# Third modulation round taken from the gated products into three heads, with its weights packed in order of use

## The chip, the core and the metric

The kernel runs on one core of one Trainium2 chip. The metric is the device time of one execution in microseconds; the median of several runs is given. Engines are named as in the profile: PE (TensorE matmul), PEld (TensorE weight load), DVE (VectorE), ACT (ScalarE), POOL (GpSimd), SP (SyncE, which issues most loads).

## What is computed

Two blocks of a network on 512 positions of width 1024. The change lies in the first one. All of it that matters here:

```python
cond = jax.nn.silu(c)
mod = cond @ ada_w[l] + ada_b[l]                       # (1, 6 * 1024)
sh1, sc1, g1, sh2, sc2, g2 = jnp.split(mod[:, None, :], N_MOD, axis=-1)
u = rms_norm(x, mix_pre_g[l]) * (1.0 + sc1) + sh1
proj = u @ w_in[l]                                     # heads (q, k, v, o), gates, glu
...                                                    # 4 heads of a chunkwise mLSTM
a, gt = jnp.split(glu, 2, axis=-1)
y = causal_dwconv(a * jax.nn.sigmoid(gt), cv_dw_w[l], cv_dw_b[l])   # 31 taps
y = jax.nn.silu(layer_norm(y, cv_ln_g[l], cv_ln_b[l]))
mix = jnp.concatenate([h, y], axis=-1) @ w_out[l]
x = x + g1 * rms_norm(mix, mix_post_g[l])
u = rms_norm(x, ffn_pre_g[l]) * (1.0 + sc2) + sh2
...                                                    # feed-forward part, uses g2 at its end
```

The second block (attention, memory cross-attention, mixture of experts) follows on the same core.

## The kernel before

**Order of the stages.** Memory keys and values (`memory`, to about 77 us), norm of x into u, the eight gated products (phase `glu`, c = 0 to 7), the gates, four heads (phases `qk`, `vo`, `mlstm`; h = 0 to 3), output product of the mixer (`wout`), feed-forward part, and then the second block. The program is straight-line. The order on each engine is set when it is built, by a scheduler that mostly follows the order of the code but takes an instruction earlier where its data should be ready.

**Modulation rounds.** `mod` has 6144 columns, in three rounds of 2048 (`ada_round`, r = 0, 1, 2). A round has eight steps, one for each 128 rows of `ada_w`. A step loads two tiles of 128 x 1024 floats (512 KB each, SP) and multiplies them with the condition in four matmuls (eight records in the profile, line L245), which lie in four column strips of PE and add up in one PSUM bank `pb` over all eight steps. At the end DVE adds the bias (L248) into `misc`. The tiles have four buffers, so two steps can be loaded ahead. Round 0 runs within the memory stage. Rounds 1 and 2 run within the gated products: there the tiles have the tag "qk" of the pool `pa`, and the biases lie in two tiles of that pool. The pool's space is that of the pool of the memory stage and is free once the last result of that stage is stored (`kvd`). c = 0, 1, 4, 5 take one step each, and c = 2, 3, 6, 7 take three.

**Weights of products.** `weight` loads 512 KB (tag "raw", three buffers, SP). In the stages around the change ACT writes the rounded high part (L133) and the negative raw value (L135) is made into the low part by an accumulating transfer that POOL issues (L136). The pairs have four buffers ("whl"). `fm_tile` makes one product of 128 x 512 outputs of them: 24 matmuls (L144, L145, L146). One c of the gated products is two such products, pg and pv, and DVE multiplies them to g (L647).

**Convolution.** The 31 taps over g are a generator: each step is one DVE instruction (L630) on an accumulator y. `pump(n)` issues n steps; `PUMP` says how many after each c (first eight numbers), each qk product (ninth) and each vo weight (tenth). What is left is issued at once by `drain` in head 3.

**Heads.** A head has four qk products, then four weights for v and the output gate (kk = 0 to 3, into four PSUM banks), the scores between them, and the matmuls with v (`mlstm_out`). The results of two heads lie in one half of hT.

**Large tiles.** xT (x transposed), u, hT and yT take two halves each of a tag "U" with four buffers (`U`, `Uh`), which rotate. `sh2` and `g2p`, columns of rounds 1 and 2, are taken in head 1.

Of the kernel before, what the change touches and what calls it, by code (L numbers as in the profile page):

```python
# [11 lines left out]
F32 = mybir.dt.float32  # L12
F32R = mybir.dt.float32r
# [3 lines left out]
ALU = mybir.AluOpType  # L17
PSUM = bass.MemoryType.PSUM

P = 128  # L20
# [26 lines left out]
class Kern:  # L47
    def __init__(self, ctx, tc, a, cidx):
        self.ctx, self.tc, self.nc, self.a, self.cidx = ctx, tc, tc.nc, a, cidx
        self.uid = 0  # L50
        self.phase = "a"
        self.bg = []

        self.lowdma = False
        self.turn = 0
# [36 lines left out]
    def Uh(self, dt):  # L92
        return self.p0.tile([P, 4, 2, 512], dt, tag="U", bufs=4, name=self.nm("U"))
# [135 lines left out]
    def ada_round(self, r, pool, tag, bias=None):  # L229

        nc = self.nc
        if bias is None:
            bias = self.tB()
        for j in range(4):
            o = r * 2048 + j * 512
            nc.sync.dma_start(bias[32 * j:32 * j + 32, :], self.a["ada_b"][0:1, o:o + 512].partition_broadcast(32))
        ps = self.psB()
        for k in range(8):
            w = []
            for j in range(2):  # L240
                t = pool.tile([P, 1024], F32, tag=tag, bufs=4, name=self.nm("aw"))
                nc.sync.dma_start(t, self.a["ada_w"][k * P:(k + 1) * P, r * 2048 + j * 1024:r * 2048 + (j + 1) * 1024])
                w += [t[:, :512], t[:, 512:]]
            for j in range(4):
                nc.tensor.matmul(ps[32 * j:32 * j + 32, :], self.crep[:, k, :], w[j], start=k == 0, stop=k == 7)  # L245
            yield
        self.mods[r] = self.misc[:, r % 2 * 512:r % 2 * 512 + 512]
        nc.vector.tensor_tensor(self.mods[r], ps, bias, op=ALU.add)  # L248
        yield
# [242 lines left out]
    def block1(self):  # L492
        nc, tc, a = self.nc, self.tc, self.a
        self.ada_setup()
        with tc.tile_pool(name="pz", bufs=1) as pz:
# [19 lines left out]
            ada = self.ada_round(0, pz, "aw")  # L515
# [13 lines left out]
            def weave(i):  # L529
                if i in (0, 2, 3, 5, 7, 9, 11, 13):  # L530
                    next(ada, None)
                if i == 13:
                    next(ada, None)
                if i in (3, 5, 7, 9):
                    x_load((3, 5, 7, 9).index(i))
                if i == 15:
                    norm1()
# [4 lines left out]
        with tc.tile_pool(name="pf", bufs=1) as pf:  # L542
# [4 lines left out]
            for tb in range(4):  # L547
                t = pf.tile([P, 1024], F32, tag="x4", bufs=6, name=self.nm("x"))
# [63 lines left out]
    def mixer(self, pa, u):  # L612
        nc, a = self.nc, self.a
# [20 lines left out]
        PUMP = (8, 9, 10, 10, 10, 10, 10, 10, 6, 6)  # L634
        self.lowdma = True
        self.phase = "glu"
        bias = [pa.tile([P, n], F32, tag=t, bufs=1, name=f"adab{t}")[:, :512] for t, n in (("dec", 1280), ("og", 1024))]
        adas = [self.ada_round(r + 1, pa, "qk", bias[r]) for r in range(2)]
        for c in range(8):
# [3 lines left out]
            for _ in range((0, 0, 1, 2)[c % 4]):  # L643
                next(adas[c // 4])
# [5 lines left out]
            for _ in range((1, 1, 2, 1)[c % 4]):  # L650
                next(adas[c // 4])
            if c == 5:
                next(adas[0])
# [3 lines left out]
        next(adas[1])  # L657
        hT = self.U()
        wi = 17
        for h in range(4):  # L660
            self.phase = "qk"
            qk = []
            for i in range(4):
# [14 lines left out]
                if i == 0 and h:  # L678
                    turn()
# [9 lines left out]
            for kk in range(4):  # L689
# [8 lines left out]
                self.pump(PUMP[9])  # L698
                if h == 3:
                    next(norm)  # L700
# [3 lines left out]
                if kk == 1 and h == 1:  # L704
                    sh2 = self.mod_col8(1, 1)
                    g2p = self.mod_col8(2, 0, "ffn_pre_g")
# [1320 lines left out]
def layout(i):  # L2027
    d = {}
    d["cols"], idx = cols_pack(i)
    d["c"] = np.ascontiguousarray(i["c"].reshape(8, P).T)  # L2030
    d["ada_w"] = i["ada_w"][0]
# [76 lines left out]
```

## Time and profile before

| | |
|---|---|
| median of 3 runs | 1599.25 us (1596.74 to 1600.09) |
| profiled execution | 1592.64 us |
| its span, first to last instruction | 1590.9 us |
| mean granted clock of TensorE | 0.990 |
| gated products, first matmul to the first of the gates | 79.81 to 209.81 us |
| gates and heads 0 to 2 | 209.81 to 389 us |

In the rows below a time is in microseconds from the start of the span. A wait is put down to the one that came last. "PEclk" is the granted clock of TensorE as a share of 2.4 GHz, and "DMA" or "DMA share" is the mean busy share of the 16 DMA engines, whose queues are counted packet by packet, so that it can exceed 1 slightly.

### The profile page before, as it was taken

What the parts mean: (1) busy time and instruction counts of PE and PEld (TensorE: products, weight loads), DVE (VectorE), ACT (ScalarE), POOL (GpSimd) and SP (SyncE); (2) the same over time, 40 slices, a digit from 0 to 9 for tenths busy, and PEclk for the clock granted to TensorE, in tenths of its full rate; (3) what the DMA queues carried; (4) which work ended last, traced back from release to release, by engine and by line L of the source; (5) the groups of instructions that cost most, each with busy time, mean ns of one, the idle gap of its engine ahead of it and who ended that gap; (6) DMA issues with size and microseconds to landing.
All of it is one profiled execution on the core that took longest, in us unless ns stands there. A gap on an engine that the chain in (4) does not pass through costs nothing.

```text
span 1590.9 us, 20242 instructions
## 1 busy us (share of the span) xinstructions
PE 1529.4 (96%) x7272; PEld 1115.5 (70%) x7272; DVE 1029.1 (65%) x2189; ACT 680.1 (43%) x1227; POOL 106.8 (7%) x137
## 2 busy tenths in 40 slices
PE   7998899999999999999999999999999989999997
PEld 5665578888888888888888877878877864444432
DVE  4576669998766865656525777857667375565543
ACT  5542276676766744444324454445355221111110
POOL 1111111111000000000000020101010010000000
PEclk9999999999999999999999999999999999999998
DMA  8899967666476433222436542532334789999931
GB/s 324 292 272 305 285 161 173 158 156 148 121 253 209 135 115 97 93 93 94 137 119 200 173 119 82 159 113 87 128 124 159 257 300 381 414 417 417 417 136 54
DMA packets 90586, 313.39 MB, mean 197 GB/s; under 512 B 10609, under 2 KB 11121, under 8 KB 90481
## 3 DMA queue, kind: packets, MB, share of 16 engines
q1 hardware_dynamic: 77808, 268.00, 47.9%
q0 software_dynamic: 9792, 35.66, 10.0%
q10 hardware_dynamic: 2880, 8.39, 1.4%
q8 instruction: 58, 0.95, 0.3%
q14 instruction: 48, 0.39, 0.1%
HBM read 271.64 MB, written 14.68 MB: 180 GB/s over the span
## 4 chain that ended last, share of the span: by engine, by line
PE 82%; DVE 7%; DMA 4%; ACT 2%; issue 2%; POOL 2%; SPq 1%; ACTq 0%; DVEq 0%; POOLq 0%
PE moe_pa L1852 7%; PE up_pa L146 5%; PE up_pa L145 5%; PE up_pa L144 5%; PE moe_pb L1891 4%; PE moe_pa L1877 4%; PE vo_pa L144 2%; PE vo_pa L146 2%; PE vo_pa L145 2%; PE wout_pa L146 2%; PE wout_pa L144 2%; PE wout_pa L145 2%; PE glu_pa L144 1%; DMA glu_aw<-in_ada_w_dram 1%; PE glu_pa L146 1%
## 5 line engine op out<-in xcount | busy, mean ns | idle before, releaser
L630 DVE SCALAR_TENSOR_TENSOR y<-g,cols,y 128x503 f32<-128x503 f32 (+18 forms) x240 | 167.1, 727 | 5.2 <-ACT y L627 3.0
L146 PE MATMUL up_pa<-u,up_w 128*128 128x512 f32 (+1 forms) x384 | 145.6, 380 | 0.0
L145 PE MATMUL up_pa<-u,up_w 128*128 128x512 f32 (+1 forms) x384 | 144.1, 376 | 0.4 <-DVE u L187 0.4
L144 PE MATMUL up_pa<-u,up_w 128*128 128x512 f32 (+1 forms) x384 | 143.2, 374 | 0.3 <-ACT u L186 0.3
L1892 DVE TENSOR_TENSOR crossq_U<-crossq_U,moe_pb 128x512 f32<-128x512 f32 x120 | 76.0, 681 | 84.2 <-PE moe_pb L1891 84.2
L909 DVE SCALAR_TENSOR_TENSOR up_tA<-up_pa,cols,up_tA 128x511 f32<-128x511 f32 x88 | 65.8, 749 | 78.6 <-ACT up_tA L907 77.1
L145 PEld LDWEIGHTS up_pa<-u,up_w 128*128 128x128 f32 x384 | 72.1, 188 | 16.3 <-DVE u L187 0.6
L144 PEld LDWEIGHTS up_pa<-u,up_w 128*128 128x128 f32 x384 | 71.8, 188 | 15.5 <-ACT u L186 1.1
L146 PEld LDWEIGHTS up_pa<-u,up_w 128*128 128x128 f32 x384 | 72.2, 188 | 13.7
L139 DVE TENSOR_TENSOR down_w<-down_raw,down_w 128x1024 fp32r<-128x1024 f32 x36 | 42.8, 1219 | 56.0 <-ACT down_w L133 56.0
L1891 PE MATMUL moe_pb<-moe_y,moe_back 128*128 128x512 f32 x240 | 72.5, 420 | 0.7 <-ACT moe_y L186 0.7
L139 DVE TENSOR_TENSOR wout_w<-wout_raw,wout_w 128x512 fp32r<-128x512 f32 (+1 forms) x72 | 51.5, 745 | 33.0 <-ACT wout_w L133 33.0
L1854 ACT ACTIVATE moe_sl<-moe_pa,moe_gt 128x256 f32<-128x256 f32 x16 | 7.6, 473 | 146.6 <-PE moe_pa L1852 146.6
L1891 PEld LDWEIGHTS moe_pb<-moe_y,moe_back 128*128 128x128 f32 x240 | 41.4, 188 | 37.3 <-issue 25.2
L907 ACT ACTIVATE up_tA<-up_pa,cols 128x512 f32<-128x512 f32 x44 | 34.2, 777 | 72.2 <-PE up_pa L146 72.2
L133 ACT CAST down_w<-down_raw 128x1024 fp32r<-128x1024 f32 x36 | 36.6, 1049 | 64.9 <-PE down_pb L146 32.1
L133 ACT CAST wout_w<-wout_raw 128x512 fp32r<-128x512 f32 (+1 forms) x72 | 44.7, 670 | 40.9 <-PE wout_pa L146 18.8
L144 PE MATMUL glu_pa<-mem_U,glu_w 128*128 128x512 f32 x128 | 51.1, 405 | 4.4 <-ACT mem_U L186 4.4
L139 DVE TENSOR_TENSOR up_w<-up_raw,up_w 128x1024 fp32r<-128x1024 f32 (+1 forms) x48 | 54.0, 1126 | 0.2 <-ACT up_w L133 0.2
L186 ACT CAST moe_y<-moe_pa 128x512 fp32r<-128x512 f32 x32 | 18.6, 586 | 82.0 <-PE moe_pa L1877 82.0
L145 PE MATMUL g_pa<-g_w,down_U 128*128 128x512 f32 x128 | 51.0, 399 | 0.5 <-DVE g_w L139 0.5
L144 PE MATMUL g_pa<-g_w,down_U 128*128 128x512 f32 x128 | 51.3, 402 | 0.0
(731 smaller groups left out, 4070.7 us busy)
## 6 DMA issues: line engine op xcount, KB each, us to landing
up_raw<-in_ffn_up_dram SPq DMA_DIRECT2D x44, 512.0 KB, 3.6
wout_raw<-in_w_out_dram SPq DMA_DIRECT2D x40, 512.0 KB, 3.6
down_raw<-in_ffn_down_dram SPq DMA_DIRECT2D x36, 512.0 KB, 4.2
ew<-in_w_gu_dram SPq DMA_DIRECT2D x35, 512.0 KB, 9.6
glu_aw<-in_ada_w_dram SPq DMA_DIRECT2D x32, 512.0 KB, 7.0
wo_ew<-in_w_gu_dram SPq DMA_DIRECT2D x17, 512.0 KB, 9.9
mem_raw<-in_w_kv_dram SPq DMA_DIRECT2D x16, 512.0 KB, 5.8
mem_aw<-in_ada_w_dram SPq DMA_DIRECT2D x16, 512.0 KB, 7.0
```

The source lines that it names most:

```text
L133: nc.scalar.copy(w[:, 0, c], raw[:, c])
L139: nc.vector.tensor_tensor(w[:, 1, c], raw[:, c], w[:, 0, c].bitcast(F32), op=ALU.subtract)
L144: mm(out, lh, rh, start=start, stop=False)
L145: mm(out, lh, rl, start=False, stop=False)
L146: mm(out, ll, rh, start=False, stop=stop)
L630: nc.vector.scalar_tensor_tensor(acc[:, s:], g[:, :512 - s], cw[:, j:j + 1], acc[:, s:], op0=ALU.mult, op1=ALU.add)
L907: nc.scalar.activation(acc, pq, AF.Identity, scale=cwv(2), bias=self.col("ffn_conv_b", cc))
L909: nc.vector.scalar_tensor_tensor(acc[:, s:], pq[:, :512 - s], cwv(2 - s), acc[:, s:], op0=ALU.mult, op1=ALU.add)
L1852: nc.tensor.matmul(ps[r, :], s["xT"][:, k, r], w[j][k // 2][:, (k % 2) * 512:(k % 2 + 1) * 512], start=k == 0, stop=k == 7)
L1877: nc.tensor.matmul(pd[h][r, :], s["aT"][:, f, r], w[j][4 + f][:, h * 512:(h + 1) * 512], start=f == 0, stop=f == 1)
L1891: nc.tensor.matmul(pc, back[:, tb * P:(tb + 1) * P], y[:, i, c], start=i == 0, stop=i == 1)
L1892: nc.vector.tensor_tensor(self.xs[tb][:, c], self.xs[tb][:, c], pc, op=ALU.add)
```

## The change

- Rounds 1 and 2 no longer run side by side with their steps in clusters. Round 1 takes one step after each c of the gated products. Round 2 runs in the heads, in four groups of two steps: after kk = 3 of head 0, kk = 1 and kk = 3 of head 1, and kk = 1 of head 2.
- A round can be cut into groups: each group adds up in a PSUM bank of its own, and DVE adds it to the result so far. Round 2 has four such groups.
- The bias is loaded straight into the result in `misc`, and the sum is added to it there.
- The tiles of rounds 1 and 2 are the four quarters of one half of tag "U": the one that held the second half of xT and later holds the second half of hT. To fix which, the four buffers become four tags U0 to U3 of one buffer each, taken in turn.
- `ada_w` is laid out by the host as (round, step, tile), so that one tile is 512 KB in one piece; before, its 128 rows of 4 KB lay 24 KB apart.
- More convolution steps are issued after each c (98 in all instead of 77) and fewer after each qk product (5 instead of 6).
- `sh2` and `g2p` are taken in head 3.

```diff
     def Uh(self, dt):
-        return self.p0.tile([P, 4, 2, 512], dt, tag="U", bufs=4, name=self.nm("U"))
+        self.turn_u += 1
+        return self.p0.tile([P, 4, 2, 512], dt, tag=f"U{self.turn_u % 4}", bufs=1, name=self.nm("U"))
...
+    def ada_round(self, r, tiles, groups=(8,)):
+        nc = self.nc
+        mods = self.mods[r] = self.misc[:, r % 2 * 512:r % 2 * 512 + 512]
         for j in range(4):
             o = r * 2048 + j * 512
-            nc.sync.dma_start(bias[32 * j:32 * j + 32, :], self.a["ada_b"][0:1, o:o + 512].partition_broadcast(32))
...
+            nc.sync.dma_start(mods[32 * j:32 * j + 32, :], self.a["ada_b"][0:1, o:o + 512].partition_broadcast(32))
+        k = 0
+        for n in groups:
+            ps = self.psB()
+            for i in range(n):
+                w = []
+                for j in range(2):
+                    t = tiles()
+                    nc.sync.dma_start(t, self.a["ada_w"][r, k, j])
+                    w += [t[:, :512], t[:, 512:]]
+                for j in range(4):
+                    nc.tensor.matmul(ps[32 * j:32 * j + 32, :], self.crep[:, k, :], w[j], start=i == 0, stop=i == n - 1)
+                k += 1
+                if i == n - 1:
+                    nc.vector.tensor_tensor(mods, ps, mods, op=ALU.add)
+                yield
...
-        PUMP = (8, 9, 10, 10, 10, 10, 10, 10, 6, 6)
+        PUMP = (8, 12, 13, 13, 13, 13, 13, 13, 5, 6)
         self.lowdma = True
         self.phase = "glu"
-        bias = [pa.tile([P, n], F32, tag=t, bufs=1, name=f"adab{t}")[:, :512] for t, n in (("dec", 1280), ("og", 1024))]
-        adas = [self.ada_round(r + 1, pa, "qk", bias[r]) for r in range(2)]
+        hT = Halves([self.Uh(F32R)])
+        aw = Halves([self.Uh(F32)])
+        turns = [0]
+        def tiles():
+            turns[0] += 1
+            return aw.rows(turns[0] % 4)
+        ada = self.ada_round(1, tiles)
         for c in range(8):
             pg = self.fm_tile(u, self.weight(W[2 * c]), self.psA())
             th = self.tA()
             nc.scalar.activation(th, pg, AF.Tanh, scale=0.5)
-            for _ in range((0, 0, 1, 2)[c % 4]):
-                next(adas[c // 4])
             pv = self.fm_tile(u, self.weight(W[2 * c + 1]), self.psA())
...
             self.pump(PUMP[c])
-            for _ in range((1, 1, 2, 1)[c % 4]):
-                next(adas[c // 4])
-            if c == 5:
-                next(adas[0])
+            next(ada)
...
-        next(adas[1])
-        hT = self.U()
+        ada = self.ada_round(2, tiles, (2, 2, 2, 2))
...
+                    if h == 3:
+                        self.turn_u -= 1
+                        hT.t.append(self.Uh(F32R))
                     turn()
...
                 self.pump(PUMP[9])
+                if (h, kk) in ((0, 3), (1, 1), (1, 3), (2, 1)):
+                    next(ada)
+                    next(ada)
...
-                if kk == 1 and h == 1:
+                if kk == 1 and h == 3:
                     sh2 = self.mod_col8(1, 1)
                     g2p = self.mod_col8(2, 0, "ffn_pre_g")
...
-    d["ada_w"] = i["ada_w"][0]
+    d["ada_w"] = np.ascontiguousarray(i["ada_w"][0].reshape(8, P, 3, 2, 1024).transpose(2, 0, 3, 1, 4))
```

## Rows read from the trace of the kernel before

**Rows 1.** The page: the chain that ended last, by engine.

```profile
PE 82%; DVE 7%; DMA 4%; ACT 2%; issue 2%; POOL 2%; SPq 1%; ACTq 0%; DVEq 0%; POOLq 0%
```

**Rows 2.** Windows: stretch, length, busy of PE, PEld, DVE, ACT, POOL, PEclk, DMA share, GB/s.

```profile
79.81:97.46 17.65, 14.02 (x57) 9.12 (x57) 9.38 (x19) 9.04 (x13) 2.73 (x5) 1.00 1.01 273
97.46:147.37 49.91, 44.11 (x194) 28.01 (x192) 36.94 (x54) 14.28 (x16) 5.16 (x6) 0.93 0.98 293
147.37:171.68 24.31, 24.31 (x113) 18.25 (x113) 6.86 (x10) 9.00 (x10) 3.44 (x4) 1.00 0.97 270
171.68:209.81 38.13, 33.76 (x153) 19.46 (x153) 23.97 (x33) 10.55 (x12) 3.44 (x4) 0.96 0.91 274
...
215.40:389.00 173.60, 172.62 (x830) 142.78 (x829) 165.43 (x345) 122.72 (x204) 22.36 (x26) 1.00 0.65 158
```

**Rows 3.** Waits of PE, 79.8 to 215.4 and 215.4 to 432: us, times, longest.

```profile
PE glu_pb L245 <- DMA glu_aw<-in_ada_w_dram: 10.7, 4, 5.5
PE glu_pa L144 <- ACT mem_U L186: 4.4, 2, 2.9
...
PE vo_pa L144 <- DVE qk_tA L671: 1.0, 1, 1.0
```

**Rows 4.** Timeline of PE in the gated products: start, us, instruction, idle before.

```profile
96.48 1.05 PE L245 MATMUL glu_pb<-glu_aw,misc 128*32 128x512 f32 x4 [0.69 <-DMA glu_aw<-in_ada_w_dram]
...
129.66 3.17 PE L245 MATMUL glu_pb<-glu_aw,misc 128*32 128x512 f32 x8 [5.46 <-DMA glu_aw<-in_ada_w_dram]
...
191.07 3.19 PE L245 MATMUL glu_pb<-glu_aw,misc 128*32 128x512 f32 x8 [4.37 <-DMA glu_aw<-in_ada_w_dram]
...
209.81 0.50 PE L144 MATMUL gates_pa<-mem_U,gates_w 128*128 128x512 f32 x1
```

**Rows 5.** Waits of SP's queue, 0 to 240.

```profile
SPq L242 <- PE glu_pb L245: 18.7, 12, 3.8
```

**Rows 6.** Timeline of PE: the steps after c = 3 and, two c later, after c = 5.

```profile
147.37 1.15 PE L245 MATMUL glu_pb<-glu_aw,misc 128*32 128x512 f32 x8
...
171.68 1.06 PE L245 MATMUL glu_pb<-glu_aw,misc 128*32 128x512 f32 x8
```

**Rows 7.** Timelines of DVE and SP around the start of the gated products.

```profile
89.35 0.54 DVE L525 TENSOR_SCALAR norm_tB<-mem_U,norm_mcol,norm_mcol 128x512 f32<-128x512 f32 x1
...
88.39 3.69 SPq L242 DMA_DIRECT2D glu_aw<-in_ada_w_dram  x4
```

**Rows 8.** DMA from 80 to 210: queue (packets, MB, share); loads with us to landing.

```profile
q1 hardware_dynamic: 7593, 26.78, 58.9%
...
glu_w<-glu_raw POOLq DMA_DIRECT2D x14, 512.0 KB, 8.6
glu_raw<-in_w_in_dram SPq DMA_DIRECT2D x12, 512.0 KB, 4.7
```

**Rows 9.** Tile `glu_aw`: its 32 issues in ns, its landings, min/median/max.

```profile
L242 SPq DMA_DIRECT2D glu_aw<-in_ada_w_dram x32: 327/383/1685, 88.4 to 201.6; - x32
...
DMA to landing us min/median/max: 3.8/7.0/8.4
```

**Rows 10.** Timelines of POOL and PE: a vo low part, issued and first used.

```profile
278.35 0.86 POOL L136 DMA_DIRECT2D vo_w<-vo_raw  x1 [7.66 <-ACT vo_w L135]
...
292.45 0.39 PE L144 MATMUL vo_pa<-vo_w,mem_U 128*128 128x512 f32 x1
```

**Rows 11.** DMA from 240 to 390: the accumulating transfers of the heads.

```profile
qk_w<-qk_raw POOLq DMA_DIRECT2D x12, 512.0 KB, 4.8
```

**Rows 12.** Line L630 from 79.8 to 215: count, ns min/median/max.

```profile
L630 DVE SCALAR_TENSOR_TENSOR y<-g,cols,y x97: 709/734/753, 96.5 to 215.0; 128x511 f32<-128x511 f32 x5, 128x510 f32<-128x510 f32 x5, 128x509 f32<-128x509 f32 x4, 128x508 f32<-128x508 f32 x4
```

**Rows 13.** Timeline of DVE: the addition at the end of a round.

```profile
149.15 0.68 DVE L248 TENSOR_TENSOR misc<-glu_pb,adabdec 128x512 f32<-128x512 f32 x1
```

**Rows 14.** Waits of PE from 0 to 79.8: the only one for a load.

```profile
PE mem_pb L431 <- DMA m<-in_mem_dram: 7.4, 2, 6.4
```

**Rows 15.** Waits of SP's queue from 1000 on: the experts' loads (L1735).

```profile
SPq L1735 <- PE moe_pa L1877: 68.9, 28, 8.9
```

More of the change, by code (lines that the diff above doesn't have):

```diff
@@ L52, in __init__ @@
         self.bg = []
+        self.turn_u = -1
         self.lowdma = False
@@ L227, in ada_setup @@
         self.mods = {}
-    def ada_round(self, r, pool, tag, bias=None):
+    def ada_round(self, r, tiles, groups=(8,)):
         nc = self.nc
-        if bias is None:
-            bias = self.tB()
+        mods = self.mods[r] = self.misc[:, r % 2 * 512:r % 2 * 512 + 512]
         for j in range(4):
             o = r * 2048 + j * 512
-            nc.sync.dma_start(bias[32 * j:32 * j + 32, :], self.a["ada_b"][0:1, o:o + 512].partition_broadcast(32))
[L237 to L249, printed above, removed]
+            nc.sync.dma_start(mods[32 * j:32 * j + 32, :], self.a["ada_b"][0:1, o:o + 512].partition_broadcast(32))
[14 more added lines that the diff above has]
+                yield
     def mod_cols(self, r):
@@ L513, in x_load @@
                         xT[:, i * 4:i * 4 + 4, 0, tb * P:(tb + 1) * P], ps.rearrange("p (k t) -> p k t", k=4))
-            ada = self.ada_round(0, pz, "aw")
+            ada = self.ada_round(0, lambda: pz.tile([P, 1024], F32, tag="aw", bufs=4, name=self.nm("aw")))
             u = self.U()
@@ L530, in weave @@
                 if i in (0, 2, 3, 5, 7, 9, 11, 13):
-                    next(ada, None)
-                if i == 13:
                     next(ada, None)
```

## The prediction

> **What bounds the kernel now.** I read the page first: PE carries 82% of the chain that ended last [rows 1]. So the question is where PE is not fed. The windows by stage answer it [rows 2]: in the heads PE is back to back (172.62 busy of 173.60 us), but the gated products lose time in three of their four stretches. The waits of PE in that stage name one cause: 10.7 us for `glu_aw`, the modulation weights, beside 4.4 us for u at its start [rows 3]. The timeline shows where: a step of a modulation round (8 matmul records, 1.06 us when its data is there [rows 6]) comes after 5.46 us of idling at 129.66 and 4.37 us at 191.07, and then takes 3.17 and 3.19 us [rows 4]. The granted clock of those two stretches is 0.93 and 0.96, while it is 1.00 in the others [rows 2]: after the idling, part of the stretch ran at 1.2 GHz instead of 2.4. Why the data is late: each of c = 2, 3, 6 and 7 takes three steps and the other c one, through four tiles, which is two steps; SP waited 18.7 us for `glu_pb` before it could issue the next loads [rows 5], while the DMA engines were 91 to 101% busy [rows 2].
>
> Where there is one step per c, nothing is lost: from 147.37 to 171.68 two whole c take 24.31 us [rows 6], and PE is busy 24.31 of 24.31 us with the DMA share at 0.97 [rows 2].
>
> **The change, part by part.** The sum is made against the profiled execution, 1592.64 us (a span of 1590.9 and 1.74 around it). The median of the runs is 1599.25, 6.6 above it; I carry the difference over to the median.
>
> *First c.* The aw tiles now lie in the second half of xT, which the norm reads until 89.35 + 0.54 = 89.89 us [rows 7]; before, they lay in a pool that came free earlier, and SP issued the first four from 88.39 [rows 7]. So the first step's two loads start about 89.9 + 0.8 of issue (two of 0.38 [rows 9]), and land 7.0 us later (median of 32 in this stage [rows 9]), at 97.7; with 1.06 us for the step the first c ends at 98.8 instead of 97.46, where the next window starts [rows 2] (its second half started at 96.48 [rows 4]): +1.3. Bounds: a landing of 8.4, the longest [rows 9], makes it +2.7; one of 4.7, that of `glu_raw` in the same stage [rows 8], makes it -1.0.
>
> *c = 1 to 7.* Each has exactly one step, with its loads free to start two c ahead. I price each at (171.68 - 147.37) / 2 = 12.16 us [rows 6]: 85.1 us, so that the stage ends at 98.8 + 85.1 = 183.9. Before, gates start at 209.81 [rows 4]: -25.9 us. The gates' own product (to 215.40, 5.59 us) moves along unchanged.
>
> *Can the DMA engines keep up?* Their work from 79.81 to 209.81 is 17.65 x 1.01 + 49.91 x 0.98 + 24.31 x 0.97 + 38.13 x 0.91 = 125.0 us at full share [rows 2]. The hardware queue takes 58.9% of 130 us for 26.78 MB, 2.86 us per MB [rows 8]; the 16 loads that leave are 8.39 MB, 24.0 us. 101.0 us of work remain for a path of 104.1 (79.81 to 183.9): a share of 0.97, at which rows 2 show no idling. If DMA nevertheless ended last, at that share the stage would take 101.0 / 0.97 = 104.1. Both limits agree, so there is little more to gain here and little to lose.
>
> *Heads.* The eight steps of the third round now stand in four groups of two, after kk = 3 of head 0, kk = 1 and 3 of head 1 and kk = 1 of head 2. PE has no room there [rows 2], so they count in full: 8 x 1.06 = 8.5 us. Where the two halves of a step are issued apart, 4 records cost 1.05 and the step 2.1 [rows 4]: at most 8.5 more. I take 8.5, since loads that start a head earlier are there together. Their loads start without a wait except in one place: those of (1, 3) need the tiles of (1, 1), two weights of kk earlier, and two products take 12.16 - 1.06 = 11.1 us [rows 6]. Four issues of 0.38 and the longest landing, 8.4, are 9.9 [rows 9]. It just fits; if their 2.1 MB move at half the rate of rows 8, beside accumulations, they take 12.0 us and cost 1.3 with the first issue.
>
> *Weights behind those loads.* SP issues in order, so the raw weights queue behind 2.1 MB, 6.0 us at 2.86 us per MB. The tightest low part I find is issued at 278.35 and used at 292.45 [rows 10]; such a landing takes 4.8 us here [rows 11], so 9.3 us are spare, and 5.5 remain if the landing takes the 8.6 of the saturated stage [rows 8], or 3.3 if it is 6.0 late; both together would cost 0.5. Zero in the sum. The DMA share of the heads, 0.65 [rows 2], rises by 24.0 us over 182, to about 0.75.
>
> The Trainium skill, "DMA: Bandwidth & Descriptors", section "Queues, rings and completion order", says that each engine takes turns between the queue rows it has work for, a packet at a time. So a burst of loads would slow the accumulating transfers (POOL's queue) while it lasts, rather than hold them back to its end. The trace agrees so far: the same accumulation takes 8.6 us beside a full load queue and 4.8 in the heads [rows 8, 11]. By that rule a burst costs each accumulation about 3.8 us, within the spare 9.3, and the sum stays.
>
> *VectorE.* 21 more convolution steps lie in the gated products (98 of 240 instead of 77). At 0.734 us each [rows 12], 13 per c and the like for g are 10.3 us, below 12.16; nobody there waits for y. In the heads 4 fewer per head (44 instead of 48) leave room for the adds, now one per group instead of one in all, 0.68 each [rows 13]. That cover matters: VectorE is busy 165.43 of 173.60 us there [rows 2], but PE waited for it once, 1.0 us [rows 3]. I price this at 0; between -1.0 (that wait goes) and +2.7 (all four adds uncovered).
>
> *Bias and packing.* Biases go straight to the result tile, as many small loads as before and two tiles fewer to wait for: hidden. Contiguous weights: 128 rows of 4 KB a tile either way. Round 0 in the memory stage cannot gain from faster loads: PE's only wait for a load there is for the memory rows [rows 14]. In the gated products the loads start two c ahead. So 0, and at best the -1.0 of the first c above. Fixed tags for U follow the order in which four buffers rotated before; `sh2` and `g2p` move two heads later at the same cost. 0.
>
> *After the heads* all waits are for PE's own progress, down to the experts' loads (their issue waits for `moe_pa` [rows 15]), so the rest shifts as it is.
>
> Sum: +1.3 and 85.1 against 112.35 (97.46 to 209.81) give -25.9; +8.5 in the heads: **-17.4 us**. 1592.64 becomes 1575.2, and the median 1599.25 becomes 1581.8.
>
> **The rivals.**
> *The heads stutter.* Late aw or late weights make PE idle 2 to 3 us at each of the four groups, 8 to 12 us. For: PE has no slack, (1, 3) fits by 1.2 us. Against: spare times of 9.3 us. Total about -7.4: 1592.
> *Slower.* Each group comes as late as the bad steps do now: 5.46 idle plus 3.17 - 1.06 = 2.11 at the low clock, 7.6 each [rows 4], 30.3 in all; -17.4 + 30.3 = +12.9: 1612. It decides from 17.4 / 4 = 4.4 us per group. Against: three groups have loads that can start a whole head ahead.
> *More is gained.* The timed runs are 6.6 us above the profiled one; if that lies in the same waits for aw, they go too: -24: 1575.
> *The change does not spread the steps.* Engine orders come from the scheduler, by its own idea of when data is ready. If it puts the first step where it idles 5.46 us and comes back cold, 7.6 are lost: -9.8: 1589.5.
>
> **How the numbers follow.** Forecast 0.53 (own range 1576 to 1588), stuttering 0.20, more 0.15, not spread 0.06, slower 0.06. The range takes in stuttering and the larger gain, and leaves out the slower rival and their tails: 1572 to 1593. A measurement of this kernel tells some 0.2%, 3.2 us, from no change. Faster by more: all but the slower rival and a part of the stuttering, 0.88; within it 0.06; slower 0.06.
>
> **What would show it.** PE waits for `glu_aw` fall from 10.7 to under 3 us; granted clock 1.00 from c = 1 to gates; gates start near 184; head 0's first product near 189.5 instead of 215.4; from there to the mixer's output product the distance grows by 8.5. Wrong if the c take over 12.5 us each (DMA), if PE idles beside the new `pb` groups, or if a later stage gives back what was gained.

## The result and the profile after

The changed kernel takes 1577.42 us (median of 4 runs, 1576.65 to 1579.63), the kernel before 1597.99 beside it: a ratio of 0.9877, 95% interval 0.9853 to 0.9901, or -20.6 us. Measured once more (`a2_after_again` below) it was 1579.14 against 1596.25, a ratio of 0.9896 (0.9881 to 0.9911), or -17.1. The forecast was 1581.8, or -17.4.

The profiled execution of the changed kernel took 1578.05 us with a span of 1576.3, against 1592.64 and 1590.9 before: -14.6. The profiled run of before is one of its shortest: all runs of before, beside the result and beside the experiments, lie between 1592.1 and 1601.1. So the sum below is made for -14.6, and the medians differ by 2 to 6 us more.

Line numbers of the changed kernel: a product's matmuls are L146 to L148, a modulation step L249, its loads L246, its addition L252, raw weights L131, their high part L135, the convolution over g L632 with its first tap L629, and that of q and k L675 with its first tap L673. Windows by stage, columns as in [rows 2]:

```profile
79.74:95.00 15.26, 13.63 (x53) 10.22 (x57) 7.49 (x16) 9.05 (x13) 3.10 (x5) 0.89 0.99 288
95.00:140.00 45.00, 44.93 (x209) 33.48 (x209) 41.27 (x61) 17.64 (x20) 6.04 (x8) 1.00 0.96 263
140.00:180.76 40.76, 40.76 (x192) 30.02 (x190) 34.20 (x51) 17.16 (x19) 6.02 (x7) 1.00 0.98 260
...
208.80:389.00 180.20, 177.09 (x859) 139.91 (x858) 150.13 (x315) 119.61 (x205) 22.35 (x26) 0.99 0.74 186
```

From 95.00 to the gates PE is busy 85.69 of 85.76 us at a granted clock of 1.00, where [rows 2] had idling and 0.93 and 0.96. The DMA share is still 0.96 to 0.98. (In the first stretch the clock is 0.89: the first matmuls ran at the 1.2 GHz level, to which the last section comes back.) Waits of PE from 70 to 430, beside [rows 3]:

```profile
PE vo_pa L146 <- DVE qk_tA L675: 3.1, 1, 3.1
PE glu_pa L146 <- ACT mem_U L188: 2.8, 2, 1.5
PE mlstm_pb L146 <- DVE misc L284: 0.4, 2, 0.2
PE glu_pa L147 <- DVE mem_U L189: 0.4, 1, 0.4
```

The 10.7 us for the modulation weights are gone, and a wait at the first vo product has grown from 1.0 to 3.1. Timeline of PE: the first, second and last step of the second round, the gates (beside [rows 4, 6]), and the longest of the four groups in the heads:

```profile
94.89 1.07 PE L249 MATMUL glu_pb<-glu_U,misc 128*32 128x512 f32 x8
107.13 1.07 PE L249 MATMUL glu_pb<-glu_U,misc 128*32 128x512 f32 x8
...
179.77 1.06 PE L249 MATMUL glu_pb<-glu_U,misc 128*32 128x512 f32 x8
180.76 0.50 PE L146 MATMUL gates_pa<-mem_U,gates_w 128*128 128x512 f32 x1
...
298.33 2.44 PE L249 MATMUL vo_pb<-glu_U,misc 128*32 128x512 f32 x16
```

Where the profiled 14.6 us went, by marks in the two traces (before, then after). Start of the gates: 209.81 and 180.76, **-29.05**. From there to the end of the last q/k product: 190.33 and 201.98, **+11.65**. From there to the first matmul of the mixer's output product: 34.30 and 37.07, **+2.77**. From there to the end: 1156.46 and 1156.49. The sum is -14.6. The second profile of the changed kernel divides otherwise: its gates start at 182.85, and 198.28 and 37.07 follow, so -26.96, **+7.95** and +2.77.

### The profile page after: what moved, and what is told of

Read it like the earlier page. It is cut to its first block, busy times and chain, and to the rows that moved or that the text cites. A ratio compares the mean times of both kernels' runs of the same rounds, so it can differ in the third digit from the quotient of the medians.

```text
span 1576.3 us, 20234 instructions
## 1 busy us (share of the span) xinstructions
PE 1523.0 (97%) x7272; PEld 1115.0 (71%) x7272; DVE 1030.9 (65%) x2192; ACT 681.4 (43%) x1227; POOL 107.2 (7%) x137
## 4 chain that ended last, share of the span: by engine, by line
PE 77%; DMA 8%; DVE 8%; ACT 3%; issue 2%; POOL 2%; SPq 0%; ACTq 0%; DVEq 0%; POOLq 0%
PE moe_pa L1862 7%; PE up_pa L148 5%; PE up_pa L147 5%; PE up_pa L146 5%; PE moe_pb L1901 4%; PE moe_pa L1887 4%; DMA glu_raw<-in_w_in_dram 2%; DMA glu_w<-glu_raw 2%; PE vo_pa L146 2%; PE vo_pa L148 2%; PE vo_pa L147 2%; PE wout_pa L148 2%; PE wout_pa L146 2%; PE wout_pa L147 2%; PE qk_pa L146 1%
## 5 line engine op out<-in xcount | busy, mean ns | idle before, releaser
L632 DVE SCALAR_TENSOR_TENSOR y<-g,cols,y 128x493 f32<-128x493 f32 (+26 forms) x240 | 165.7, 728 | 9.8 <-ACT y L629 8.1
L148 PE MATMUL up_pa<-u,up_w 128*128 128x512 f32 (+1 forms) x384 | 145.6, 380 | 0.0
L146 PE MATMUL up_pa<-u,up_w 128*128 128x512 f32 (+1 forms) x384 | 143.2, 374 | 0.3 <-ACT u L188 0.3
L146 PEld LDWEIGHTS up_pa<-u,up_w 128*128 128x128 f32 x384 | 71.9, 188 | 15.5 <-ACT u L188 1.1
L148 PEld LDWEIGHTS up_pa<-u,up_w 128*128 128x128 f32 x384 | 72.2, 188 | 13.7
L135 ACT CAST down_w<-down_raw 128x1024 fp32r<-128x1024 f32 x36 | 36.4, 1049 | 65.0 <-PE down_pb L148 33.7
L135 ACT CAST wout_w<-wout_raw 128x512 fp32r<-128x512 f32 (+1 forms) x72 | 44.9, 670 | 44.6 <-PE wout_pa L148 21.5
L146 PE MATMUL glu_pa<-mem_U,glu_w 128*128 128x512 f32 x128 | 50.9, 401 | 2.8 <-ACT mem_U L188 2.8
L146 PE MATMUL g_pa<-g_w,down_U 128*128 128x512 f32 x128 | 51.4, 403 | 0.0
```

The lines of the kernel that those rows point to most:

```text
L135: nc.scalar.copy(w[:, 0, c], raw[:, c])
L146: mm(out, lh, rh, start=start, stop=False)
L148: mm(out, ll, rh, start=False, stop=stop)
L632: nc.vector.scalar_tensor_tensor(acc[:, s:], g[:, :512 - s], cw[:, j:j + 1], acc[:, s:], op0=ALU.mult, op1=ALU.add)
```

## The experiments

**Was it the spread or the amount?** The change does two things to the gated products: it takes 8.4 MB of loads out and it spreads the steps that stay. Each was undone alone.

`e4_clustered`, the old clusters with the new amount:

```diff
+            for _ in range((0, 0, 1, 2, 0, 0, 0, 0)[c]):
+                next(ada)
             pv = self.fm_tile(u, self.weight(W[2 * c + 1]), self.psA())
...
-            next(ada)
+            for _ in range((1, 1, 2, 1, 0, 0, 0, 0)[c]):
+                next(ada)
```

> The changed kernel, third round still in the heads, but the eight steps of the second round clustered in the gated products as each round was before: one step for c = 0 and c = 1, three for c = 2 and c = 3, none after that. The DMA traffic is that of the changed kernel, only its spread is the old one. Theory (the clusters cost the time): PE idles for the modulation weights once or twice, 5 us each, and comes back at the low clock for 2 us, so gates start 6 to 14 us after those of the changed kernel's runs (180.8 to 183.1) and the total is 6 to 14 us above 1577. Rival (the number of loads in the stage cost the time, not their spread): no wait above 1 us for the modulation weights, gates start within 2 us, total within 3 us of 1577.

1587.41 us (1583.05 to 1591.33), ratio 0.9933 (0.9909 to 0.9957): 8 to 10 us above the changed kernel. The gates start at 194.25. The window of the bad place:

```profile
126.00:136.00 10.00, 4.76 (x12) 1.79 (x13) 9.79 (x16) 2.00 (x2) 0.86 (x1) 0.67 0.96 288
```

and PE's timeline there:

```profile
131.24 3.13 PE L249 MATMUL glu_pb<-glu_U,misc 128*32 128x512 f32 x8 [5.62 <-DMA glu_U<-in_ada_w_dram]
```

PE waits 7.5 us in all for the modulation weights, three times. This is the pattern of [rows 4] almost to the tenth (5.46 idle and 3.17 there), with half of the modulation loads. So the clusters make it without the larger amount.

`e5_both_spread`, the new spread with the old amount:

```diff
+        ada, ada2 = self.ada_round(1, tiles), self.ada_round(2, tiles)
...
+            if c:
+                next(ada if c < 5 else ada2, None)
             pv = self.fm_tile(u, self.weight(W[2 * c + 1]), self.psA())
...
-            next(ada)
+            next(ada if c < 4 else ada2)
+            if c == 7:
+                next(ada2)
```

> The changed kernel with both rounds in the gated products and none in the heads, but evenly: one step after c = 0, two for each further c, three at c = 7. The traffic of the stage is that of the kernel before, the spread that of the change. Theory (the clusters cost the time): the stage grows by the eight steps alone, 8.5 us, gates start near 190 and head lengths fall by 8 to 9, total within 3 us of 1577. Rival (the amount of DMA work, 125 us at full share, ends last): at a share of 0.97 the stage cannot end before 79.8 + 125 / 0.97 = 208.7, PE waits for weights of either kind, and the total is 15 to 20 us above 1577, that is, near the kernel before.

1592.35 us (1587.13 to 1593.61), ratio 0.9970 (0.9953 to 0.9987): 13 to 15 us above the changed kernel (the rival had 15 to 20), and 3 to 5 below before. My theory of clusters alone falls here; the rival named 208.7 as the earliest end of the stage, and the gates start at 208.58. Windows by stage:

```profile
79.80:95.00 15.20, 9.96 (x34) 7.47 (x35) 8.12 (x17) 7.18 (x11) 2.44 (x5) 0.89 1.03 290
95.00:140.00 45.00, 42.08 (x189) 27.41 (x188) 37.29 (x54) 17.74 (x20) 6.02 (x7) 0.97 1.02 299
140.00:180.00 40.00, 39.53 (x187) 27.00 (x187) 27.70 (x40) 13.99 (x17) 4.30 (x5) 0.99 0.95 277
180.00:208.58 28.58, 24.49 (x108) 14.33 (x104) 19.20 (x29) 9.54 (x11) 3.44 (x4) 0.95 1.03 298
```

Waits of PE from 70 to 440:

```profile
PE glu_pb L249 <- DMA glu_U<-in_ada_w_dram: 7.3, 5, 3.9
PE glu_pa L146 <- ACT mem_U L188: 5.7, 2, 4.2
```

The DMA engines are full in three of the four windows (0.95 in the other, where PE hardly idles), and with this amount PE waits spread as well as clustered. So the two parts need each other: by the totals, spreading alone gives 3 to 5 us and moving the loads out alone 8 to 11 (the first by the medians, the second by the ratios), both together 17 to 21. Beyond the stage, e5 has no groups in its heads, so its total is better than its gates' start says. The starts of the gates, before any group in the heads, tell it without that: 1.2 us earlier than before by spreading alone, 15.6 by moving the loads alone, 27.0 and 29.1 by both.

**What do the groups in the heads cost?** `e3_no_round2` and `e7_no_loads`:

```diff
-        ada = self.ada_round(2, tiles, (2, 2, 2, 2))
+        ada = self.ada_round(2, tiles, ())
```

> The changed kernel without the eight steps of the third modulation round: neither their loads, nor the matmuls and adds, so the third round's product is left out and only its bias stands in its place. Theory (the groups in the heads cost what PE works on them): the heads are shorter by 8.2 us (1.93 + 1.92 + 2.44 + 1.92), the total by 8 to 9. Rival (their 8.4 MB of loads cost time elsewhere too, by transfers that come late): the total is shorter by 11 us or more. The 3.1 us wait at the first vo product stays in either case, since no load of the third round stands before it that PE needs; if it goes, the loads caused it.

```diff
-                    nc.sync.dma_start(t, self.a["ada_w"][r, k, j])
+                    if r < 2:
+                        nc.sync.dma_start(t, self.a["ada_w"][r, k, j])
```

> The changed kernel with the eight steps of the third round in the heads, but without their loads: they multiply what the second round left in the tiles, so the third round's values are wrong while PE's and VectorE's work is the same. From the start of the gates to the last product of q and k the changed kernel's arrangement took 198.3 to 198.7 us in three runs without a long wait at the first vo product, and 189.3 without the third round, 9.1 less, of which PE's own work is 8.2. Theory (loads hidden): 198.3 to 198.7 us again, total within 2 us of 1577. Rival (the missing 0.9 is the price of the loads): 197.5 or less there.

1566.69 us (1564.84 to 1568.36) without the round, 1575.19 (1572.56 to 1575.47) without its loads. One window of each kernel from the start of the gates to the end of the last q/k product. Without the round:

```profile
183.05:372.38 189.33, 188.43 (x901) 155.89 (x898) 168.00 (x343) 135.79 (x223) 24.94 (x29) 1.00 0.66 158
```

With its steps but without its loads:

```profile
181.32:379.18 197.86, 196.79 (x965) 157.20 (x962) 173.14 (x350) 136.53 (x223) 24.92 (x29) 1.00 0.64 154
```

The changed kernel itself, in its second profile:

```profile
182.85:381.13 198.28, 197.34 (x965) 157.35 (x962) 172.91 (x350) 136.67 (x223) 24.97 (x29) 1.00 0.77 194
```

The steps cost 197.86 - 189.33 = 8.5 us and their loads 198.28 - 197.86 = 0.4. That lies between what the two theories expected of `e7_no_loads` (198.3 or more, and 197.5 or less), and the 0.4 is no larger than the scatter of the profiles with those loads (198.3 to 198.7), so the price of the loads is 0.4 us or nothing. The totals agree as far as they resolve it: without the round 9.5 to 11 us less than the variants beside it, without its loads a ratio of 0.9857 (0.9835 to 0.9879), whose interval overlaps that of the changed kernel.

**The new wait.** In the first profile of the changed kernel PE waits 3.10 us for the bank that the third q/k convolution of head 0 frees. Timeline of PE:

```profile
213.76 0.47 PE L146 MATMUL vo_pa<-vo_w,mem_U 128*128 128x512 f32 x1 [3.10 <-DVE qk_tA L675]
...
214.75 0.63 PE L147 MATMUL vo_pa<-vo_w,mem_U 128*128 128x512 f32 x1
215.18 0.63 PE L148 MATMUL vo_pa<-vo_w,mem_U 128*128 128x512 f32 x1
```

and the window behind the wait:

```profile
213.70:217.00 3.30, 3.24 (x9) 2.60 (x10) 3.30 (x6) 3.23 (x6) 0.87 (x2) 0.58 0.97 251
```

The matmuls start 0.43 us apart instead of 0.23, at the 1.2 GHz level (granted clock 0.58), for some 3 us. From the first to the eleventh start it is 3.95 us where `e1_no_pack` takes 2.38, so 1.6 us go on top of the wait. My first theory was that six convolution steps, which VectorE does just ahead of that convolution (three in the kernel before), cause it. Two runs change them:

```diff
-        PUMP = (8, 12, 13, 13, 13, 13, 13, 13, 5, 6)
+        PUMP = (8, 9, 10, 10, 10, 10, 10, 10, 6, 6)
```

> The changed kernel with the convolution steps spread as in the kernel before (77 in the gated products, 6 after a product of q and k) instead of 98 and 5. The changed kernel has one new wait: the first vo product of head 0 waits 3.1 us for a convolution of VectorE (before 1.0), and some ten matmuls behind it run at 427 instead of 227 ns. Theory (the steps that were moved forward stand ahead of that convolution): three steps are in front of it again, the wait falls to about 1 us, no matmuls at the low clock there, heads 3 to 4 us shorter at that place; but later heads may be covered worse, up to 2.7 us given back. Rival (the wait comes from the gates and VectorE's backlog being the same in time, whatever the steps): the wait stays at 3 us and the time is within 1 us of the changed kernel's profile.

```diff
-        PUMP = (8, 12, 13, 13, 13, 13, 13, 13, 5, 6)
+        PUMP = (8, 15, 16, 16, 16, 16, 15, 8, 5, 6)
...
-                self.pump(PUMP[8])
+                self.pump(PUMP[8] if h else 2)
```

> The changed kernel with still more convolution steps forward in the gated products (15 or 16 for most c, 8 after the last) and only two after each product of q and k in head 0. Theory (the y steps that stand ahead of the third q/k convolution of head 0 cause the 3.1 us wait of PE and the cold matmuls after it): wait under 1.5 us, no matmul above 300 ns, the first vo product about 3 us earlier against the start of the gates, total 3 to 5 us below the changed kernel. Rival (VectorE has too much in c of the gated products: 16 x 0.73 = 11.7 us of 12.1 beside the products of g): g comes late, PSUM banks of pg and pv stay held, PE idles in the gated products and the gain is lost.

1576.62 us (1571.76 to 1579.66) and 1577.74 (1573.91 to 1581.98): no difference from the changed kernel. In the profiles much is as that theory expected: the wait is 1.4 and 1.2 us, and from the gates to the last q/k product it takes 198.70 and 198.27 us instead of 201.98. And yet the theory is wrong. (In `e3_no_round2` the wait is 0.9; what was put down for that run takes this as a sign that the third round's loads cause it.) `e1_no_pack`, made for another question, has the changed kernel's steps and its loads of the third round, and a wait of 1.3:

```diff
-                    nc.sync.dma_start(t, self.a["ada_w"][r, k, j])
+                    nc.sync.dma_start(t, self.a["ada_w"][k * P:(k + 1) * P, r * 2048 + j * 1024:r * 2048 + (j + 1) * 1024])
...
-    d["ada_w"] = np.ascontiguousarray(i["ada_w"][0].reshape(8, P, 3, 2, 1024).transpose(2, 0, 3, 1, 4))
+    d["ada_w"] = i["ada_w"][0]
```

> The changed kernel with the modulation weights left in their old layout (128 rows of 4 KB that lie 24 KB apart, instead of one piece of 512 KB). Theory (the packing is worth nothing): gated products end at 180.8 us as in the changed kernel, accumulating transfers and weight loads land as there (8.2 and 3 to 8 us), time within 3 us of 1577.4. Rival (a part of the gain is the packing): loads move slower, waits for the modulation weights come back, gates start later than 182 us, and the norm-to-first-step path (-1.6 us against 12.16 + before) is given back.

1576.17 us (1574.95 to 1579.60), ratio 0.9877, the same as with packing. The packing is worth nothing that can be measured. (Its gates start at 183.09, later than the 182 that the rival named, but so do those of the changed kernel in its second profile, at 182.85.)

The second theory: VectorE starts late, since the first taps of the convolution are ScalarE's and stand there behind weights that have not landed.

```diff
-            nc.scalar.activation(acc, g, AF.Identity, scale=cw[:, 30 * 8 + c:30 * 8 + c + 1], bias=self.col("cv_dw_b", c))
+            nc.vector.tensor_scalar(acc, g, cw[:, 30 * 8 + c:30 * 8 + c + 1], self.col("cv_dw_b", c), op0=ALU.mult, op1=ALU.add)
```

> The changed kernel with the first tap of each of the eight convolutions made by VectorE instead of ScalarE. In the profile of the changed kernel VectorE idles 8.1 us for those eight instructions, because ScalarE is held, in order, by weights that have not landed; VectorE is then busy without a gap to the first vo product of head 0, which waits 3.1 us for it. Theory (that is where the wait starts): the idling for the first tap goes, VectorE does 8 x 0.4 = 3.2 us more, the third q/k convolution of head 0 no longer holds PE for over 1.5 us, no matmuls at the low clock there, total 0 to 4 us below 1577. Rival (VectorE's amount of work, not its start, sets the wait): 3.2 us more work make the wait longer than 3.1 us.

1578.15 us (1576.28 to 1582.33). The wait is 5.6 us, so this theory falls; but not for the rival's reason either, since VectorE was idle. One line each of the timelines of ScalarE, VectorE and PE:

```profile
195.22 1.05 ACT L135 CAST qk_w<-qk_raw 128x1024 fp32r<-128x1024 f32 x1 [5.76 <-DMA qk_raw<-in_w_in_dram]
...
200.53 0.75 DVE L675 SCALAR_TENSOR_TENSOR qk_tA<-qk_pa,cols,qk_tA 128x511 f32<-128x511 f32 x1 [6.85 <-ACT qk_tA L673]
...
219.18 0.76 PE L146 MATMUL vo_pa<-vo_w,mem_U 128*128 128x512 f32 x1 [5.55 <-DVE qk_tA L675]
```

This shows the chain. On ScalarE the cast of the fourth q/k weight of head 0 stands ahead of most of the gates' activations and of all first taps of q and k. When its raw weight is late, the whole chain of ScalarE and VectorE behind it is. The start of that cast, in the profiles with the changed kernel's order in head 0, and before:

| kernel | gates start | cast starts, after the gates' start | of it waiting for the load | bank free, after the cast | PE waits |
|---|---|---|---|---|---|
| before | 209.81 | 7.17 | 0 | 24.18 | 0.98 |
| after | 180.76 | 9.37 | 1.94 | 23.63 | 3.10 |
| after, second profile | 182.85 | 7.18 | 0 | 23.65 | 0.94 |
| e1_no_pack | 183.09 | 7.43 | 0.28 | 23.73 | 1.26 |
| e3_no_round2 | 183.05 | 7.18 | 0 | 23.61 | 0.90 |
| e6_free_bank | 181.61 | 7.17 | 0 | 23.65 | 1.16 |
| e7_no_loads | 181.32 | 7.17 | 0 | 23.79 | 1.06 |
| e8_dve_init | 182.00 | 13.22 | 5.76 | 23.96 | 5.55 |

The bank comes free 23.6 to 24.2 us after the cast, whatever VectorE has to do in between, and the wait exceeds 1.0 us by about as much as the cast is late (in `e8_dve_init` by less, since PE itself was held 1.2 us earlier for a q/k weight). `e4_clustered` and `e5_both_spread`, with other gated products ahead, fit it less well: the bank comes free 24.1 and 23.0 us after the cast, PE waits 1.6 and 0.5, and neither cast waits for its load. (In `e2_old_pump` the cast is on time as well, at 190.12, and PE waits 1.45 us for the high part of a vo weight.) In the timeline of SP in the changed kernel a pair of the third round's loads stands right ahead of that weight:

```profile
178.10 0.86 SPq L246 DMA_DIRECT2D glu_U<-in_ada_w_dram  x2
180.14 0.33 SPq L131 DMA_DIRECT2D qk_raw<-in_w_in_dram  x1
```

and ScalarE's timeline, at the same weight:

```profile
190.13 1.05 ACT L135 CAST qk_w<-qk_raw 128x1024 fp32r<-128x1024 f32 x1 [1.94 <-DMA qk_raw<-in_w_in_dram]
```

Behind such a pair that load took 5.5, 7.3 and 9.8 us to land (e2, e6, e1), and 4.0 without the third round's loads (e3). How early it was issued counts as well: 0.62 us before the gates' start here and 2.42 after it in e8, but 2.5 to 4.6 before it in a2, e1, e2, e3, e6 and e7. To see whether the account holds, the kernel was run again as it is, and with those loads held back:

> The changed kernel once more, unaltered, for a second profile beside the two below. The wait of PE at the first vo product of head 0 was 3.10, 1.26, 1.45, 1.16, 1.06 and 5.55 us in the profiles of the changed kernel and its variants, and in each the bank came free 23.6 to 24.0 us after ScalarE began to cast the fourth weight of head 0. Theory (that cast is late only where the weight lands late, behind the first loads of the third round): a wait of 1.0 us plus as much as the cast begins later than 7.2 us after the start of the gates, so between 1.0 and 5.6 here too. Rival (VectorE's convolution steps set it): the wait does not follow the cast. Time 1576 to 1579 by either.

1579.14 us (1578.62 to 1579.88). The cast was on time, the wait 0.94, and no matmul at that place slow: it follows the cast. The timelines of SP and ScalarE, beside the lines above:

```profile
177.84 0.97 SPq L246 DMA_DIRECT2D glu_U<-in_ada_w_dram  x2
179.88 0.33 SPq L131 DMA_DIRECT2D qk_raw<-in_w_in_dram  x1
...
190.03 1.05 ACT L135 CAST qk_w<-qk_raw 128x1024 fp32r<-128x1024 f32 x1
```

But the load was no faster. It took 10.0 us and landed at 189.87, 0.16 before ScalarE was ready for it; in the first profile the cast could begin at 190.13. What differs is the start of the gates, 180.76 there and 182.85 here. So the wait of the first profile is what its shorter first c had gained, given back: PE came 2.1 us earlier to a weight that came at the same time. Only the 1.6 us of slow matmuls are lost on top.

```diff
                 qk.append(t)
+                if i == 0 and not h:
+                    for j in range(4):
+                        nc.vector.tensor_copy(aw.rows(j)[:, :1], acc[:, :1])
                 self.pump(PUMP[8])
```

> The changed kernel with the first four loads of the third round held back until the first q/k product of head 0 is through its convolution (VectorE writes one column of each tile first), so that they are issued behind the raw weights of head 0 instead of between them. Theory (those loads make the fourth weight land 5.5 to 10 us after its issue instead of 4.0 without them): it lands in 4 to 6 us, ScalarE casts it 7.2 us after the start of the gates, the first vo product waits 1.0 to 1.1 us, no cold matmuls there, and the runs lie 0 to 2 us below the changed kernel's. Rival (the lateness comes from the accumulating transfers at the end of the gated products): landing stays at 7 to 10 us and the wait between 1.2 and 5.6.

1577.87 us (1576.28 to 1579.26), the same as the kernel beside it within the spread. The load, issued at 179.68, lands in 6.5 us, between the two expectations (in `e10_gates` below, with the same loads held back, in 4.4); the cast is on time (189.89). But head 0 is now arranged otherwise, and waits appear that were not there:

```profile
PE mlstm_pb L146 <- DVE mlstm_sm L829: 1.0, 1, 1.0
PE mlstm_pb L849 <- DVE qk_tA L675: 0.6, 1, 0.6
...
PE vo_pa L146 <- DVE qk_tA L675: 0.3, 1, 0.3
```

From the gates to the last q/k product it takes 200.09 us, against 198.28 and 201.98 in the two profiles of the changed kernel: the gate takes 1.9 us from the bad case and adds 1.8 to the good one.

**The first c.** The last run also holds back the second pair of the second round's loads:

```diff
+            if c == 0:
+                for j in (3, 0):
+                    nc.vector.tensor_copy(aw.rows(j)[:, :1], th[:, :1])
             pv = self.fm_tile(u, self.weight(W[2 * c + 1]), self.psA())
```

> As the run with the third round's first loads held back, and the second pair of loads of the second round also held back, until the first product of c = 0 is in ScalarE (about 91 us instead of 84.7). Theory (that pair competes with the raw weights of c = 0 and c = 1, for which ScalarE waits 3.6 and 7.2 us in the changed kernel's profile): the wait for u or for the low part of the second weight at c = 0 (1.3 to 3.4 us, or 2.0 us, in all profiles so far) shrinks by 1 to 2 us, total 1 to 3 us below the run before. Rival (the stage is limited by the amount of traffic from 80 us on): what is gained at c = 0 comes back as a wait for the modulation weights at c = 1, no change.

1577.06 us (1573.81 to 1581.59): no difference. ScalarE still waits 4.03 us for a raw weight at 86.06, with the second half of u behind it, and the gates start at 182.41, as in the others. So that pair is not what makes the weight late; what does is not settled. PE no longer waits for the low part of a weight near the end of the first c (2.1 us at 96.82 in e9), but it waits for one later, where no other profile with one step after each c has a wait:

```profile
122.33 0.50 PE L148 MATMUL glu_pa<-mem_U,glu_w 128*128 128x512 f32 x1 [1.45 <-DMA glu_w<-glu_raw]
```

That is much as the rival had it, though the rival named the modulation weights.

No version that does all of the work was faster than the changed kernel by more than its runs scatter.

## Why the prediction was right, and where it was not

*c = 1 to 7* (12.16 us each): right. The steps come 12.11 us apart, from 107.13 to 179.77, and PE idles nowhere between.

*Can the DMA engines keep up* (101.0 us of work in 104.1): right. The work was 15.26 x 0.99 + 45.00 x 0.96 + 40.76 x 0.98 = 98.2 us in 101.0, a share of 0.97. `e5_both_spread` shows the edge itself, where the DMA engines decide. That its end came within 0.1 us of the 208.7 worked out from 125 us at 0.97 is luck: the trace has a share of 1.00 over 128.78 us, so there was more work, done at a higher share.

*First c* (+1.3): the wait was the right one, the time of its end was not. The aw loads do start when the norm has read the second half of xT, but that is not at 89.89 as before [rows 7]. In the changed kernel VectorE makes these reads (L529) in two groups of four, and the last ends at 84.65; in the kernel before, the last one came by itself, at 89.35, behind other work. Timeline of VectorE, timeline of SP and waits of SP:

```profile
82.74 1.91 DVE L529 TENSOR_SCALAR norm_tB<-mem_U,norm_mcol,norm_mcol 128x512 f32<-128x512 f32 x4
...
84.67 2.95 SPq L246 DMA_DIRECT2D glu_U<-in_ada_w_dram  x4
...
SPq L246 <- DVE norm_tB L529: 1.9, 1, 1.9
```

With the 0.8 and 7.0 of the prediction the first step's data would be there at about 92.5 (an estimate), ahead of the step at 94.89, and PE has no wait for it in any profile with this arrangement. Nine of them (in `e10_gates` a later wait moves the gates) have their gates' start between 180.76 and 183.09, 182.3 in the mean; less 7 x 12.11 the first c ends between 96.0 and 98.3, 97.5 in the mean, which is where it ended before (97.46). What PE waits for there is the second half of u (0.9 to 3.4 us in eight of the nine), in the first profile behind a raw weight that ScalarE casts ahead of it, and in five of them the low part of a weight (1.9 to 2.2 us). So the term is about 0, and it scatters by more than 1 us. In the first profile it was -1.5, or 2.8 below the forecast: most of the 3.1 us by which the gates started earlier than forecast.

*Heads* (8.5): right. 8.5 for the steps, at most 0.4 for the loads. The (1, 3) group, which "just fits", took 2.44 us where the others took 1.92 and 1.93: 0.5 of the 1.3 allowed for.

*Weights behind those loads* (0): the mechanism was the right one, the place was wrong. I looked for the tightest low part in the later heads [rows 10, 11], where nothing came of it. The load that suffers is a high part in head 0, issued while the gated products still fill the DMA engines. Its price is 0 to 0.3 us in most profiles, but 2.1 us of wait and 1.6 us of matmuls at the low clock in the first one, and more in `e8_dve_init`. With a pair of modulation loads ahead of it on SP's queue it took 5.5 to 10.0 us to land, without one 4.0, 4.4 and 6.5 (e3, e10, e9). That the pair alone decides is not shown: the two ranges overlap, and in a2, e2 and e6 the weight was in time behind such a pair. The Trainium skill, "DMA: Bandwidth & Descriptors", section "Queues, rings and completion order", which the prediction cites for turns between queues, also says that on each engine the descriptors of one ring are consumed in the ring's order, though a later one may finish its write first. The landing times just given fit it. The prediction's DMA share for the heads was added up wrongly: 0.65 + 24.0 / 182 is 0.78, not 0.75. The second profile has 0.77.

*VectorE* (0): right, and better founded now. Moving the steps forward or back makes no difference that the runs resolve, and the wait that looked like VectorE's was ScalarE's, standing for a load.

*Bias and packing* (0): right for the packing. `sh2` and `g2p` were said to move at the same cost, which they do: the heads are 1.0 us shorter for it up to the last q/k product (189.33 without the round against 190.33 before), and 0.9 us longer behind it.

*After the heads* ("shifts as it is"): not quite. Between the last q/k product and the mixer's output product 2.8 us were added: 0.9 of them are the moved `sh2` and `g2p`, 0.4 the waits for `misc` shown above. Of the other 1.5, 0.84 comes from the mark: seven matmuls of the last head (435.36 to 436.20 in the trace before) stood behind the first four of the output product and now stand ahead of them. The remaining 0.7 was not taken apart. The stretch is 37.0 to 37.1 us in all twelve profiles of the changed kernel and its variants, also without the third round (e3) and with the old convolution steps (e2), so neither of these makes it. The prediction's sign for all of this was a distance from head 0's first product to the mixer's output product that grows by 8.5; it grew by 14.4 in the first profile and by 10.7 in the second.

The profiled sum was -17.4 and came out at -14.6. The gated products gained 3.1 us more than forecast, the heads cost 3.1 more (3.7 for the late weight, 0.4 for the loads, less 1.0 for `sh2` and `g2p`), and 2.8 were added behind them. The first two cancel, and in part not by accident: the 2.1 us that the first profile gained in its first c against the second came back as the wait. That the medians, -20.6 and -17.1, lie so near to -17.4 is in part luck: what the profiles lack to the forecast, the timed runs of before lost beyond their profile. *More is gained* had that excess in the waits for aw. The medians fell by 20.6 and 17.1 where the profiles fell by 14.6, which points its way, but what the timed runs of before lost more than the profiled one is in no trace, so it stays argued. The rival *the heads stutter* did not come: one stall of 3.1 us, in one place and one profile of two.

## What to carry to other kernels

Where a stage's DMA engines are full, ask two questions apart: does the traffic fit at all, and does it come in time. Only both answers together gave the gain here. And an engine that casts what a load brings makes every instruction behind that cast, in its own order, wait for the load. So follow a wait through the engine that seems to cause it to the first instruction that waited for a transfer, before moving any work.

## What was not expected

After idling 3.10 us PE had the 1.2 GHz level for some 3 us (granted clock 0.58 from 213.70 to 217.00), as after 5.46 and 4.37 us in [rows 4]. After the waits of 0.9 to 1.5 us at the same place the matmuls in the other profiles stayed 0.23 us apart. But the length of the last wait does not decide it alone: before its first gated product PE idled 1.49 us in both profiles of the changed kernel, and the granted clock from 79 to 85 us was 0.72 in the first (matmuls 0.43 us apart) and 1.00 in the second. The windows of the first and of the second profile:

```profile
79.00:85.00 6.00, 4.91 (x13) 3.63 (x14) 5.64 (x12) 3.14 (x5) 0.28 (x1) 0.72 0.99 273
...
79.00:85.00 6.00, 4.45 (x17) 3.04 (x17) 6.00 (x12) 3.14 (x5) 0.56 (x1) 1.00 1.02 273
```

The same kernel lost 3.7 us at one place in one profile and nothing in another, though the load behind it landed within 0.3 us of the same time in both: the time was lost where PE had come there earlier. A single trace of each kernel would have blamed VectorE, and two experiments agreed with that by chance.
